# Loading a dense block's u columns and v rows side by side, by one transfer of 8 KB per partition

## The chip, the cores and the metric

The kernel runs on one core of one Trainium2 chip. The time is that of one execution on the device, in microseconds. Three runs of the kernel before gave 4152.92, 4156.69 and 4169.66 us; the median, 4156.69, is the time to which the changed kernel is held.

A core has five engines that take their instructions in order: PE (matmul; PEld is its weight load), DVE (elementwise work), ACT (activation functions, also copies), POOL (here it issues the gathers) and SP (here it issues most loads and stores). Sixteen DMA engines move the data of all queues.

## The reference

A diffusion trunk of two layers runs over 128 context tokens and 512 latent tokens. Each layer normalises, mixes tokens by three parallel head groups, and then lets each token pick single-neuron experts. This case is about the last step, which with its variables shortened reads:

```python
def peer_ffn(h, wq, k1, k2, u, v):                   # u, v: 16384 experts x 1024
    q = (xt @ wq).reshape(n, 8, 128)                 # 8 heads
    s1 = einsum('thd,hnd->thn', q[..., :64], k1)     # 128 keys for each half
    s2 = einsum('thd,hnd->thn', q[..., 64:], k2)
    v1, i1 = top_k(s1, 16); v2, i2 = top_k(s2, 16)
    cand = v1[..., :, None] + v2[..., None, :]       # 256 candidates per head
    top, pos = top_k(cand, 16)
    idx = (i1 * 128 + i2) at pos                     # 16 experts per head and token
    g = softmax(top)
    act = gelu(einsum('td,thkd->thk', x, u[idx]))
    return einsum('thk,thkd->td', g * act, v[idx])
```

So each token reads 128 rows of u and 128 rows of v, chosen by its own data.

## The kernel before

`peer` handles the experts of the 640 tokens in two ways at once. For the first 256 tokens (`TG`) it gathers: for each of the 128 slots a GpSimd indirect DMA (L751) brings 128 rows of 8 KB, one per token, each row an expert's u and v beside each other in the array `uv`. DVE then forms the dot product with the token (L754), ACT the gelu (L756), and DVE adds the weighted v part to `gacc` (L763). There are 4 gather buffers (`NUV`), so a gather can start only when an earlier buffer has been used up by L763.

For the other 384 tokens (`TD`) it is dense: `dense(b)` runs over 128 blocks of 128 experts. It loads the transposed u columns of a block (`raw<-uT`, 512 KB, 4 KB per partition), splits them into a rounded part and a rest (`split`: ACT writes `uhi` in L836, DVE writes `ulo` in L837), and forms all 128 x 384 products on PE (L857 to L859). After gelu (L861) DVE multiplies by the gate array `gres` (L862), which is zero for experts that a token didn't choose. Then it loads the v rows of the block (`raw<-uv`, 512 KB, the second 4 KB of each 8 KB row of `uv`), splits them in the same way into `vhi` and `vlo`, and PE adds the product to `acc` (L877).

Both loads are `dma_start` on SP's queue, into a pool of 4 buffers of 4 KB per partition (`NRAW`), u and v in turn. A load waits until `split` has read the buffer of two blocks ago. The gate array is too large to stay: a stage ahead of the dense loop (`build`, L776 to L802) makes it from one-hot matmuls, keeps a part in `gres` and writes the rest to device memory (`gsp<-sg`, on SP's queue), from where `gres<-gsp` loads on ACT's queue bring it back.

In the dense loop one block and one pump of two gathers alternate (`pump`, `issue_after(gates[...])`). The order on each engine is made by a list scheduler that the framework runs on the program; the pools decide which bytes a tile takes, and a tile waits for the earlier tiles on the same bytes (`reuse_waits="tile"`). `ixT`, `gT` and `iota8` are inputs of `build`: the chosen key indices of the dense tokens, their gates, and a ramp of 128 numbers repeated 8 times.

Of the kernel before, what the change touches and what calls it, by code (L numbers as in the profile page):

```python
# [10 lines left out]
F32 = mybir.dt.float32  # L11
# [4 lines left out]
BF16 = mybir.dt.bfloat16  # L16
F16 = mybir.dt.float16
AF = mybir.ActivationFunctionType
OP = mybir.AluOpType
# [3 lines left out]
D = 1024  # L23
TP, TS = 128, 512
T = TP + TS
L = 2
# [3 lines left out]
NEXP = 16384  # L30
# [14 lines left out]
TD = T - TG  # L45
NT_D = TD // 128
# [6 lines left out]
NUV = 4  # L53
NADA = 2
UAFT = 2
NRAW = 4
NCV = 1
ADAE = 10
ADAP = 3
# [10 lines left out]
class Trunk:  # L70
    def __init__(self, ctx, tc, I, O):
        self.tc, self.nc, self.I, self.O = tc, tc.nc, I, O
        nc = tc.nc
        self.V, self.S, self.G, self.PE = nc.vector, nc.scalar, nc.gpsimd, nc.tensor
        V, S = self.V, self.S
        pers = ctx.enter_context(tc.tile_pool(name="pers", bufs=1))
        consts = pers
        self.xT = xT = pers.tile([128, 8, T], F32, name="xT")
        for k in range(0, 8, 2):
            nc.sync.dma_start(xT[:, k:k + 2, :], I["xT"][k * 128:k * 128 + 256].rearrange("(k p) t -> p k t", p=128))  # L80

        def const(name, shape, dt=F32):
            t = consts.tile(shape, dt, name=name)
            nc.scalar.dma_start(t, I[name])
            return t

        self.vec = const("vec", [128, L, NVEC])
        self.ident = const("ident", [128, 128])
        self.nstep = consts.tile([128, 16], F16, name="nstep16")
        self.thr = consts.tile([128, 2, 16], F16, name="thr16")  # L90
        self.iota = consts.tile([128, 128], BF16, name="iota16")
        self.iota8 = consts.tile([128, 128, 8], BF16, name="iota8")
        self.lmask = consts.tile([128, 7, 128], U8, name="lmask8")
        self.sc = consts.tile([128, 8, 2], F32, name="sc")
        with tc.tile_pool(name="init", bufs=1) as ip:
            for name, shape, dst, dt in (("cT", [128, 8, 2], None, F32), ("lmask", [128, 7, 128], self.lmask, I32),
                                         ("thr", [128, 2, 16], self.thr, F32), ("nstep", [128, 16], self.nstep, F32),
                                         ("iota", [128, 128], self.iota, F32)):
                t = ip.tile(shape, dt, name="i_" + name)
                nc.scalar.dma_start(t, I[name])  # L100
                if dst is None:
                    S.activation(self.sc, t, AF.Silu)
                else:
                    V.tensor_copy(dst, t)
        V.tensor_copy(self.iota8, self.iota[:, :, None].to_broadcast([128, 128, 8]))
        self.eps = consts.tile([128, 1], F32, name="eps")
        V.memset(self.eps, EPS)
        self.one = consts.tile([128, 1], F32, name="one")
        V.memset(self.one, 1.0)
        self.ones = consts.tile([128, 128], F32, name="ones")  # L110
        V.memset(self.ones, 1.0 / D)
        self.identr = consts.tile([128, 128], F32R, name="identr")
        V.tensor_copy(self.identr, self.ident)
        self.ada = [consts.tile([128, 48, 2], F32, name=f"ada{l}") for l in range(L)]
        self.adap = ctx.enter_context(tc.tile_pool(name="adap", bufs=1))
        self.mod = [consts.tile([128, 2, 8, 2], F32, name=f"mod{l}") for l in range(L)]
# [455 lines left out]
    def peer(self, l):  # L572
        tc, nc, I = self.tc, self.nc, self.I
        V, S, G, PE = self.V, self.S, self.G, self.PE
# [4 lines left out]
        gat = self.pool(st, f"gat{l}", side="right")  # L579
        ht = [gat.tile([128, D], F32, name=f"ht{t}") for t in range(2)]  # L580
        gidx = [gat.tile([128, 128], U32, name=f"gidx{t}") for t in range(2)]
        gg = [gat.tile([128, 128], F32, name=f"gg{t}") for t in range(2)]
        ixT = gat.tile([128, 2, TD], BF16, name="ixT")
        gT = gat.tile([128, TD], F32, name="gT")

        self.psj = self.pool(st, f"psjp{l}", 2, PSUM)
        ks = self.pool(st, f"ks{l}", 1)
# [3 lines left out]
        psb = self.pool(f2, f"psbp{l}", 2, PSUM)  # L591
        self.pss = pss = self.pool(f2, f"pssp{l}", 4, PSUM)
        kp = self.pool(f2, f"tk{l}", 1)
        f1 = ExitStack()
        self.wp = self.pool(f1, f"wpp{l}", 2)
        self.tmp = self.pool(f1, f"tmpp{l}", 2)
# [138 lines left out]
        gpool = self.pool(st, f"G{l}", side="right")  # L735
        gres = gpool.tile([128, NR, NTC, GB, TC], F32, name="gres")
        bp = self.pool(f2, f"gb{l}", 2)
        self.wp = bp

        ga = {}  # L740
# [35 lines left out]
        def build(tcn):  # L776
            sg = bp.tile([128, NSP, GB, TC], F32, name="sg", tag="sg")
            for t8 in range(0, TC, 8):
                t0 = tcn * TC + t8
                ohp = bp.tile([128, 8, 128], F32, name="ohp", tag="ohp")  # L780
                ohq = bp.tile([128, 128, 8], BF16, name="ohq", tag="ohq")
                V.tensor_tensor(ohp, ixT[:, 0, t0:t0 + 8, None].to_broadcast([128, 8, 128]),
                                self.iota[:, None, :].to_broadcast([128, 8, 128]), op=OP.is_equal)
                V.tensor_tensor(ohq, ixT[:, 1, None, t0:t0 + 8].to_broadcast([128, 128, 8]), self.iota8, op=OP.is_equal)  # L784
                for t4 in range(0, 8, 4):
                    qg = bp.tile([128, 4, 128], F32, name="qg", tag="qg", bufs=NQG)
                    for t in range(4):
                        S.activation(qg[:, t, :], ohq[:, :, t4 + t], AF.Copy, scale=gT[:, t0 + t4 + t:t0 + t4 + t + 1])  # L788
                    ps = pss.tile([128, 4, 128], F32, name="ps_g", tag="s")
                    for t in range(4):  # L790
                        PE.matmul(ps[:, t, :], qg[:, t, :], ohp[:, t4 + t, :], start=True, stop=True)  # L791
                    tt = t8 + t4
                    S.activation(gres[:, :, tcn, :, tt:tt + 4],
                                 ps[:, :, :NR * GB].rearrange("p t (r b) -> p r b t", r=NR), AF.Copy)
                    so, sp = sg[:, :, :, tt:tt + 4].rearrange("p r b t -> p (r b) t"), ps[:, :, NR * GB:].rearrange("p t b -> p b t")
                    if (tt // 4) % 4 < EVD:
                        V.tensor_copy(so, sp)
                    else:
                        S.activation(so, sp, AF.Copy)  # L799
                for _ in range(NADA):  # L800
                    next(ada, None)
            nc.sync.dma_start(gsp[:, :, tcn].rearrange("r p b t -> p r (b t)"), sg.rearrange("p r b t -> p r (b t)"))  # L802
# [21 lines left out]
        uvp = {n: self.pool(st, f"uv{n}{l}", b) for n, b in (("r", NRAW), ("u", UVB["u"]), ("v", UVB["v"]))}  # L824
        awp = self.pool(st, f"aw{l}", 2)
        acc = pacc.tile([128, NT_D, 2, 512], F32, name="acc")

        def load(src):
            raw = uvp["r"].tile([128, D], F32, name="raw", tag="raw")
            nc.sync.dma_start(raw, src)  # L830
            return raw

        def split(raw, n):
            hi = uvp[n].tile([128, D], F32R, name=n + "hi", tag=n + "hi")
            lo = uvp[n].tile([128, D], F32R, name=n + "lo", tag=n + "lo")
            S.activation(hi, raw, AF.Copy)  # L836
            V.tensor_tensor(lo, raw, hi.bitcast(F32), op=OP.subtract)  # L837
            return hi, lo

        def dense(b):  # L840
            gr, bb = divmod(b, GB)
            nx = gr + NR - 1
            if NR <= nx < NGR and bb % 2 == 0:
# [1 line left out]
                a1 = a0 + 2 * NTC // GB  # L845
                nc.scalar.dma_start(gres[:, nx % NR, a0:a1].rearrange("p a b t -> p (a b t)"),
                                    gsp[nx - NR, :, a0:a1].rearrange("p a b t -> p (a b t)"))
            raw = load(I["uT"][l, b])
            if b >= UAFT:
                with tc.issue_after(gelus[b - UAFT]):  # L850
                    uhi, ulo = split(raw, "u")
            else:
                uhi, ulo = split(raw, "u")
            ps = pa.tile([128, 512], F32, name="ps_a", tag="j")[:, :TD]
            for k in range(8):
                ks = slice(k * 128, k * 128 + 128)
# [5 lines left out]
            gate = V.tensor_tensor(w.rearrange("p (a t) -> p a t", a=NTC), w.rearrange("p (a t) -> p a t", a=NTC),  # L862
                                   gres[:, gr % NR, :, bb, :], op=OP.mult)
            gates.append(gate.ins)
            e0 = l * NEXP + b * 128
            raw = load(I["uv"][e0:e0 + 128, D:])
            whi = awp.tile([128, TD], F32R, name="whi", tag="wh")
            wlo = awp.tile([128, TD], F32R, name="wlo", tag="wl")
            S.activation(whi, w, AF.Copy)  # L869
            V.tensor_tensor(wlo, w, whi.bitcast(F32), op=OP.subtract)  # L870
            vhi, vlo = split(raw, "v")
            parts = ((whi, vhi), (whi, vlo), (wlo, vhi))
            for t in range(NT_D):
                ts = slice(t * 128, t * 128 + 128)
# [16 lines left out]
        for b in range(128):  # L891
# [3 lines left out]
            with tc.issue_after(gates[max(0, b - GLAG)]):  # L895
                while todo and left - len(todo) < left * (b + 1) / 128:
                    pump()
        oa = [uvp["r"].tile([128, D], F32, name="oa", tag="raw") for t in range(NT_D)]
        for t in range(NT_D):
            o = oa[t].rearrange("p (j d) -> p j d", j=2)  # L900
            S.activation(o[:, 0], acc[:, t, 0], AF.Copy)
# [10 lines left out]
def layout(inputs):  # L912
    a = {k: np.ascontiguousarray(np.asarray(v)) for k, v in inputs.items()}
    A = {}
# [20 lines left out]
    s, t = np.arange(128)[:, None], np.arange(128)[None, :]  # L935
# [40 lines left out]
        b = a["na_rpb"][:, :, dr + 7, np.clip(dc, -15, 15) + 15]  # L976
        bias[:, :, :, BOFF[qt][0]:BOFF[qt][0] + kn * 128] = np.where(ok, b, f32(-1e30))
    A["bias"] = bias
    A["uT"] = a["peer_u"].reshape(L, 128, 128, 8, 128).transpose(0, 1, 4, 3, 2).reshape(L, 128, 128, D)
    A["uv"] = np.concatenate([a["peer_u"], a["peer_v"]], -1).reshape(L * NEXP, 2 * D)  # L980
    return {k: np.ascontiguousarray(v) for k, v in A.items()}

# [26 lines left out]
```

## Time and profile before

| what | value |
|---|---|
| median of three runs | 4156.69 us |
| span of the profiled execution, first to last instruction | 4144.4 us (the page gives no other time of it) |
| median less span | 12.3 us |
| PE busy | 3810.6 us, 92% |
| DVE busy | 3333.9 us, 80% |
| ACT busy | 1701.2 us, 41% |
| POOL busy | 757.7 us, 18% |
| moved by DMA | 1011.89 MB in 302267 packets, mean 244 GB/s |
| q0, the gathers | 536.90 MB, 33.5% of 16 DMA engines |
| q1, SP's queue | 425.45 MB, 29.4% |
| q10, ACT's queue | 46.07 MB, 2.8% |

How to read it: the shares are averages over stages of different kinds. Each of the two layers has a mixing and selecting stage and then the dense loop, some 1130 to 1180 us long, in which the DMA engines move about 377 GB/s and PE and DVE both look nearly full. What a change in that loop is worth can only be read from the loop. A packet is what one DMA engine moves at a time, here one partition's row of a transfer.

### The profile page before, as it was taken

What the parts mean: (1) busy time and instruction counts of PE and PEld (TensorE: products, weight loads), DVE (VectorE), ACT (ScalarE), POOL (GpSimd) and SP (SyncE); (2) the same over time, 40 slices, a digit from 0 to 9 for tenths busy, and PEclk for the clock granted to TensorE, in tenths of its full rate; (3) what the DMA queues carried; (4) which work ended last, traced back from release to release, by engine and by line L of the source; (5) the groups of instructions that cost most, each with busy time, mean ns of one, the idle gap of its engine ahead of it and who ended that gap; (6) DMA issues with size and microseconds to landing.
All of it is one profiled execution on the core that took longest, in us unless ns stands there. A gap on an engine that the chain in (4) does not pass through costs nothing.

```text
span 4144.4 us, 54329 instructions
## 1 busy us (share of the span) xinstructions
PE 3810.6 (92%) x19884; PEld 3204.7 (77%) x19884; DVE 3333.9 (80%) x6618; ACT 1701.2 (41%) x3268; POOL 757.7 (18%) x532
## 2 busy tenths in 40 slices
PE   7999997888999999999989999867799999999998
PEld 4896775557888888888878988745688888888886
DVE  4762359788999999999968633988799999999997
ACT  4423332884333333333354243368633333333333
POOL 0000000002333333333300000000133333333331
PEclk8999998998999999999999999978899999999999
DMA  4124232668999999999921221023599999999995
GB/s 161 33 61 128 74 110 68 186 202 291 382 367 387 373 377 375 377 376 379 375 90 33 62 69 57 26 68 113 205 355 383 375 375 372 377 377 377 381 375 213
DMA packets 302267, 1011.89 MB, mean 244 GB/s; under 512 B 28273, under 2 KB 116721, under 8 KB 236209
## 3 DMA queue, kind: packets, MB, share of 16 engines
q0 software_dynamic: 73728, 536.90, 33.5%
q1 hardware_dynamic: 210560, 425.45, 29.4%
q10 hardware_dynamic: 17712, 46.07, 2.8%
q8 instruction: 156, 2.56, 0.2%
q14 instruction: 111, 0.90, 0.1%
HBM read 960.49 MB, written 47.84 MB: 243 GB/s over the span
## 4 chain that ended last, share of the span: by engine, by line
issue 37%; PE 29%; POOL 13%; ACT 9%; DVE 7%; DMA 5%; POOLq 0%; ACTq 0%; DVEq 0%; SPq 0%
PE ps_pj L235 13%; POOL uv L751 13%; ACT qg L788 5%; DMA uv<-uv,gidx 4%; PE ps_ada L162 2%; PE ps_lv L363 2%; PE ps_g L791 2%; PE acc L877 1%; PE npo L529 1%; ACT sg L799 1%; PE ps_s L508 1%; PE ps_ms L187 1%; ACT nt L208 1%; PE po L421 1%; PE pt L524 1%
## 5 line engine op out<-in xcount | busy, mean ns | idle before, releaser
L751 POOL DMA_INDIRECT uv<-uv,gidx x512 | 750.5, 1466 | 3317.0 <-PE ps_g L791 1766.2
L754 DVE SCALAR_TENSOR_TENSOR uv<-uv,ht 128x1024 f32<-128x1024 f32 x512 | 624.2, 1221 | 116.2 <-DMA uv<-uv,gidx 115.4
L859 PE MATMUL ps_a<-hd,ulo 128*128 128x384 f32 x2048 | 695.2, 339 | 17.8 <-DVE ulo L837 17.8
L857 PE MATMUL ps_a<-hd,uhi 128*128 128x384 f32 x2048 | 700.7, 342 | 9.6 <-ACT uhi L836 9.6
L858 PE MATMUL ps_a<-hd,uhi 128*128 128x384 f32 x2048 | 694.0, 339 | 0.0
L763 DVE SCALAR_TENSOR_TENSOR gacc<-uv,gw,gacc 128x1024 f32<-128x1024 f32 x508 | 652.5, 1284 | 15.7
L877 PE MATMUL acc<-vhi,whi 128*128 128x512 f32 x1536 | 506.2, 411 | 67.1 <-ACT whi L869 66.4
L877 PE MATMUL acc<-vhi,wlo 128*128 128x512 f32 x1536 | 486.9, 398 | 2.0 <-DVE wlo L870 1.7
L836 ACT ACTIVATE vhi<-raw 128x1024 fp32r<-128x1024 f32 x256 | 271.6, 1061 | 511.7 <-PE acc L877 496.1
L877 PE MATMUL acc<-vlo,whi 128*128 128x512 f32 x1536 | 480.0, 394 | 0.0
L859 PEld LDWEIGHTS ps_a<-hd,ulo 128*128 128x128 f32 x2048 | 388.3, 190 | 24.9 <-DVE ulo L837 22.7
L857 PEld LDWEIGHTS ps_a<-hd,uhi 128*128 128x128 f32 x2048 | 387.8, 189 | 21.2 <-ACT uhi L836 10.8
L877 PEld LDWEIGHTS acc<-vhi,whi 128*128 128x128 f32 x1536 | 271.6, 189 | 160.4 <-ACT whi L869 113.1
L858 PEld LDWEIGHTS ps_a<-hd,uhi 128*128 128x128 f32 x2048 | 387.7, 189 | 10.0
L788 ACT ACTIVATE qg<-ohq,gT 128x128 f32<-128x128 bf16 x768 | 341.3, 533 | 59.5 <-DVE ohq L784 59.5
L791 PE MATMUL ps_g<-ohp,qg 128*128 128x128 f32 x1536 | 297.9, 338 | 69.5 <-ACT qg L788 68.9
L791 PEld LDWEIGHTS ps_g<-ohp,qg 128*128 128x128 f32 x1536 | 238.4, 221 | 151.9 <-ACT qg L788 116.0
L877 PEld LDWEIGHTS acc<-vhi,wlo 128*128 128x128 f32 x1536 | 282.1, 189 | 81.7 <-DVE wlo L870 24.9
L877 PEld LDWEIGHTS acc<-vlo,whi 128*128 128x128 f32 x1536 | 290.3, 189 | 65.7
L837 DVE TENSOR_TENSOR vlo<-raw,vhi 128x1024 fp32r<-128x1024 f32 x256 | 312.1, 1219 | 13.5 <-ACT vhi L836 13.3
L756 ACT ACTIVATE gw<-dots 128x2 f32<-128x2 f32 x256 | 52.1, 203 | 646.6 <-DVE uv L754 646.4
L837 DVE TENSOR_TENSOR ulo<-raw,uhi 128x1024 fp32r<-128x1024 f32 x256 | 312.8, 1222 | 0.0
(243 smaller groups left out, 6187.5 us busy)
## 6 DMA issues: line engine op xcount, KB each, us to landing
raw<-uT SPq DMA_DIRECT2D x256, 512.0 KB, 6.4
raw<-uv SPq DMA_DIRECT2D x256, 512.0 KB, 8.4
wada<-w_ada SPq DMA_DIRECT2D x192, 256.0 KB, 3.3
gsp<-sg SPq DMA_DIRECT2D x48, 896.0 KB, 5.0
gres<-gsp ACTq DMA_DIRECT2D x112, 384.0 KB, 14.5
wraw<-w_in SPq DMA_DIRECT2D x56, 512.0 KB, 3.6
wraw<-w_out SPq DMA_DIRECT2D x16, 512.0 KB, 3.6
wraw<-wq SPq DMA_DIRECT2D x16, 512.0 KB, 4.0
```

Source lines behind the costliest of these rows:

```text
L235: self.PE.matmul(ps[j][:, :n], w[:, k, :], x[:, k, :], start=(k == 0 and i == 0), stop=(k == 7 and i == 2))
L751: G.indirect_dma_start(out=b, out_offset=None, in_=I["uv"], in_offset=bass.IndirectOffsetOnAxis(ap=gidx[t][:, s:s + 1], axis=0))
L754: V.scalar_tensor_tensor(b[:, :D], b[:, :D], 1.0, ht[t], op0=OP.mult, op1=OP.mult, accum_out=dots[:, s:s + 1])
L763: V.scalar_tensor_tensor(acc_, b[:, D:], w[:, s:s + 1], acc_, op0=OP.mult, op1=OP.add)
L788: S.activation(qg[:, t, :], ohq[:, :, t4 + t], AF.Copy, scale=gT[:, t0 + t4 + t:t0 + t4 + t + 1])
L791: PE.matmul(ps[:, t, :], qg[:, t, :], ohp[:, t4 + t, :], start=True, stop=True)
L836: S.activation(hi, raw, AF.Copy)
L837: V.tensor_tensor(lo, raw, hi.bitcast(F32), op=OP.subtract)
L857: PE.matmul(ps, uhi[:, ks], hd[0][:, k, :], start=(k == 0), stop=False)
L858: PE.matmul(ps, uhi[:, ks], hd[1][:, k, :], start=False, stop=False)
L859: PE.matmul(ps, ulo[:, ks], hd[0][:, k, :], start=False, stop=(k == 7))
L877: PE.matmul(acc[:, t, j, :], a[:, ts], x[:, j * 512:(j + 1) * 512], start=(b == 0 and i == 0), stop=(b == 127 and i == len(parts) - 1))
```

## The change

In device memory the transposed u columns of a block and its v rows are put side by side in a new array `dn`, so that a partition's 4 KB of u and 4 KB of v are one row of 8 KB. `dense` loads both by one transfer of 1 MB into a buffer of 8 KB per partition; there are 3 such buffers in place of 4 of half the size. The gathers still read `uv`.

To make room in SBUF, `iota8` is no longer kept for the whole kernel but made in each layer in a pool of the build stage, and `ixT` and `gT` move from a pool that lives as long as the gathers to one that ends with the build stage.

```diff
-NRAW = 4
+NRAW = 3
...
-        self.iota8 = consts.tile([128, 128, 8], BF16, name="iota8")
...
-        V.tensor_copy(self.iota8, self.iota[:, :, None].to_broadcast([128, 128, 8]))
...
-        ixT = gat.tile([128, 2, TD], BF16, name="ixT")
-        gT = gat.tile([128, TD], F32, name="gT")
...
         kp = self.pool(f2, f"tk{l}", 1)
+        ixT = kp.tile([128, 2, TD], BF16, name="ixT")
+        gT = kp.tile([128, TD], F32, name="gT")
...
         bp = self.pool(f2, f"gb{l}", 2)
+        iota8 = bp.tile([128, 128, 8], BF16, name="iota8", tag="iota8", bufs=1)
+        V.tensor_copy(iota8, self.iota[:, :, None].to_broadcast([128, 128, 8]))
...
-        def load(src):
-            raw = uvp["r"].tile([128, D], F32, name="raw", tag="raw")
-            nc.sync.dma_start(raw, src)
-            return raw
+        def load(b):
+            raw = uvp["r"].tile([128, 2 * D], F32, name="raw", tag="raw")
+            nc.sync.dma_start(raw, I["dn"][l, b])
+            return raw[:, :D], raw[:, D:]
...
-            raw = load(I["uT"][l, b])
+            uraw, vraw = load(b)
...
-            e0 = l * NEXP + b * 128
-            raw = load(I["uv"][e0:e0 + 128, D:])
...
-            vhi, vlo = split(raw, "v")
+            vhi, vlo = split(vraw, "v")
...
-        oa = [uvp["r"].tile([128, D], F32, name="oa", tag="raw") for t in range(NT_D)]
+        oa = [uvp["r"].tile([128, 2 * D], F32, name="oa", tag="raw")[:, :D] for t in range(NT_D)]
...
-    A["uT"] = a["peer_u"].reshape(L, 128, 128, 8, 128).transpose(0, 1, 4, 3, 2).reshape(L, 128, 128, D)
+    uT = a["peer_u"].reshape(L, 128, 128, 8, 128).transpose(0, 1, 4, 3, 2).reshape(L, 128, 128, D)
+    A["dn"] = np.concatenate([uT, a["peer_v"].reshape(L, 128, 128, D)], -1)
```

The scheduler puts some instructions in another place. SP's queue before, at the end of the build stage of layer 0 (`wada<-w_ada` loads weights of the next layer's modulation):

```order
L830 DMA raw<-uT 128x1024
L802 DMA gsp<-sg 128x14x128
L153 DMA wada<-w_ada 128x512 x2
L830 DMA raw<-uv 128x1024
L830 DMA raw<-uT 128x1024
L153 DMA wada<-w_ada 128x512
L830 DMA raw<-uv 128x1024
L153 DMA wada<-w_ada 128x512
L802 DMA gsp<-sg 128x14x128
```

The same end of the stage in the changed kernel:

```order
L802 DMA gsp<-sg 128x14x128
L151 DMA wada<-w_ada 128x512 x4
L802 DMA gsp<-sg 128x14x128
L151 DMA wada<-w_ada 128x512 x2
L802 DMA gsp<-sg 128x14x128 x4
L830 DMA raw<-dn 128x2048
L802 DMA gsp<-sg 128x14x128
L830 DMA raw<-dn 128x2048 x127
```

The first four loads stood ahead of nine stores of gates; now the first load stands ahead of the last store, and the second behind it.

SP's queue before, at the end of the build stage of layer 1:

```order
L600 DMA kk<-keys 128x2048
L216 DMA wraw<-wq 128x1024 x8
L802 DMA gsp<-sg 128x14x128 x16
L830 DMA raw<-uT 128x1024
L830 DMA raw<-uv 128x1024
L830 DMA raw<-uT 128x1024
L830 DMA raw<-uv 128x1024
L802 DMA gsp<-sg 128x14x128 x8
L830 DMA raw<-uT 128x1024
```

The same end in the changed kernel:

```order
L598 DMA kk<-keys 128x2048
L214 DMA wraw<-wq 128x1024 x8
L802 DMA gsp<-sg 128x14x128 x23
L830 DMA raw<-dn 128x2048
L802 DMA gsp<-sg 128x14x128
L830 DMA raw<-dn 128x2048 x127
```

Here, too, the loads of the first two blocks stood eight stores ahead, and now stand around the last store.

DVE before, where the dense loop of layer 0 begins (`m`, `ij`, `pf`, `mk` and `gidx` belong to the selection of the second half of the gathered tokens):

```order
L696 TENSOR_TENSOR m_9109<-mk,dl 128x2048
L837 TENSOR_TENSOR ulo<-raw,uhi 128x1024
L837 TENSOR_TENSOR vlo<-raw,vhi 128x1024
L837 TENSOR_TENSOR ulo<-raw,uhi 128x1024
L837 TENSOR_TENSOR vlo<-raw,vhi 128x1024
L691 TENSOR_TENSOR m_9109<-m_9109 128x128x8
L691 TENSOR_TENSOR m_9109<-m_9109 128x128x4
L691 TENSOR_TENSOR m_9109<-m_9109 128x128x2
L693 TENSOR_TENSOR ij<-m_9109 128x128
L715 TENSOR_TENSOR gidx_4423<-f_9129,ij 128x128
L862 TENSOR_TENSOR w<-w,gres 128x384
```

The same place in the changed kernel:

```order
L689 TENSOR_TENSOR m_9075<-m_9075 128x128x2
L691 TENSOR_TENSOR ij<-m_9075 128x128
L713 TENSOR_TENSOR gidx_4421<-f_9095,ij 128x128
L837 TENSOR_TENSOR ulo<-raw,uhi 128x1024
L837 TENSOR_TENSOR vlo<-raw,vhi 128x1024
L837 TENSOR_TENSOR ulo<-raw,uhi 128x1024
L837 TENSOR_TENSOR vlo<-raw,vhi 128x1024
L862 TENSOR_TENSOR w<-w,gres 128x384
```

The four subtractions of the first two blocks have moved behind the rest of the selection; the first gate multiplication follows either way.

## Rows read from the trace of the kernel before

**Rows 1.** Busy time by stage, inside the dense loops of both layers.

```profile
core 0: us, PE busy (x) PEld busy (x) DVE busy (x) ACT busy (x) POOL busy (x), PEclk, DMA share, GB/s
1200.00:2000.00 800.00, 772.97 (x3789) 678.00 (x3788) 743.76 (x1001) 283.61 (x450) 265.95 (x180) 1.00 0.98 377
3200.00:4000.00 800.00, 770.86 (x3771) 676.44 (x3770) 742.00 (x999) 281.84 (x448) 265.74 (x180) 1.00 0.98 377
```

**Rows 2.** DVE's waits, 1200 to 2000 us, and L754 over the whole span.

```profile
DVE uv L754 <- DMA uv<-uv,gidx: 39.8, 34, 2.9
DVE w L862 <- ACT w L861: 4.7, 20, 1.6
...
L754 DVE SCALAR_TENSOR_TENSOR uv<-uv,ht 128x1024 f32<-128x1024 f32 x512 | 624.2, 1221 | 116.2 <-DMA uv<-uv,gidx 115.4
```

**Rows 3.** DVE in order of time, one block (start, duration, engine, line).

```profile
1504.43 1.22 DVE L837 TENSOR_TENSOR vlo<-raw,vhi 128x1024 fp32r<-128x1024 f32 x1
1505.76 0.56 DVE L862 TENSOR_TENSOR w<-w,gres 128x384 f32<-128x384 f32 x1
...
1512.85 1.22 DVE L837 TENSOR_TENSOR vlo<-raw,vhi 128x1024 fp32r<-128x1024 f32 x1
```

**Rows 4.** DMA queues and issues, 1200 to 2000 us; median us to landing last.

```profile
q0 software_dynamic: 25948, 188.86, 61.0%
q1 hardware_dynamic: 25959, 94.54, 31.1%
q10 hardware_dynamic: 6338, 17.31, 5.5%
...
raw<-uT SPq DMA_DIRECT2D x91, 512.0 KB, 6.5
raw<-uv SPq DMA_DIRECT2D x90, 512.0 KB, 8.6
...
uv<-uv,gidx POOLq DMA_INDIRECT x180, 10.0
```

**Rows 5.** SP's queue, q1, 1504.8 to 1508 us, then 1508.9 to 1513.2 us.

```profile
q1 hardware_dynamic: 147, 0.52, 40.1%
...
q1 hardware_dynamic: 142, 0.53, 36.1%
```

**Rows 6.** SP's and POOL's queues in order of time, around that block.

```profile
1501.87 0.33 SPq L830 DMA_DIRECT2D raw<-uT  x1
1503.46 1.86 POOL L751 DMA_INDIRECT uv<-uv,gidx  x1 [5.26 <-DVE gacc L763]
1505.63 0.93 POOL L751 DMA_INDIRECT uv<-uv,gidx  x1 [0.30 <-issue]
1505.67 0.33 SPq L830 DMA_DIRECT2D raw<-uv  x1
```

**Rows 7.** DMA queues, 1497 to 1498 us, then 1498.6 to 1500 us.

```profile
q1 hardware_dynamic: 95, 0.38, 94.2%
q0 software_dynamic: 12, 0.02, 8.0%
...
q0 software_dynamic: 62, 0.51, 95.0%
q1 hardware_dynamic: 8, 0.02, 4.4%
```

**Rows 8.** Starts of the dense loops: ACT and DVE in order of time.

```profile
961.69 1.06 ACT L836 ACTIVATE vhi<-raw 128x1024 fp32r<-128x1024 f32 x1 [3.71 <-issue]
964.66 1.28 ACT L861 ACT_TABLE_LOAD   x1
969.14 0.56 DVE L862 TENSOR_TENSOR w<-w,gres 128x384 f32<-128x384 f32 x1 [0.47 <-ACT w L861]
...
2962.08 1.06 ACT L836 ACTIVATE vhi<-raw 128x1024 fp32r<-128x1024 f32 x1 [11.38 <-DMA gsp<-sg]
2970.11 0.55 DVE L862 TENSOR_TENSOR w<-w,gres 128x384 f32<-128x384 f32 x1
```

**Rows 9.** The copy into iota8, and two loads by row size.

```profile
L105 DVE COPY iota<-iota x1: 695/695/695, 13.2 to 13.2; 128x1024 bf16<-128x1024 bf16 x1
...
kk<-keys SPq DMA_DIRECT2D x2, 1024.0 KB, 4.9
wraw<-wq SPq DMA_DIRECT2D x16, 512.0 KB, 4.0
```

More of the change, by code (lines that the diff above doesn't have):

```diff
@@ L783, in build @@
                                 self.iota[:, None, :].to_broadcast([128, 8, 128]), op=OP.is_equal)
-                V.tensor_tensor(ohq, ixT[:, 1, None, t0:t0 + 8].to_broadcast([128, 128, 8]), self.iota8, op=OP.is_equal)
+                V.tensor_tensor(ohq, ixT[:, 1, None, t0:t0 + 8].to_broadcast([128, 128, 8]), iota8, op=OP.is_equal)
                 for t4 in range(0, 8, 4):
@@ L847, in dense @@
                                     gsp[nx - NR, :, a0:a1].rearrange("p a b t -> p (a b t)"))
-            raw = load(I["uT"][l, b])
+            uraw, vraw = load(b)
             if b >= UAFT:
                 with tc.issue_after(gelus[b - UAFT]):
-                    uhi, ulo = split(raw, "u")
+                    uhi, ulo = split(uraw, "u")
             else:
-                uhi, ulo = split(raw, "u")
+                uhi, ulo = split(uraw, "u")
             ps = pa.tile([128, 512], F32, name="ps_a", tag="j")[:, :TD]
```

## The prediction, made before the changed kernel was run

> **What bounds the kernel now.** I read the busy times by stage first, since the change touches only the dense loops. In both loops DVE is busy 743 of 800 us, PE 771 to 773 at full granted clock, and the DMA engines 98% of the time at 377 GB/s [rows 1]. Three resources near their end can't be told apart by shares, so the waits come next. DVE, which runs in order, waits for one thing that counts: the gathered rows, 39.8 us in 34 pieces in 800 us, and 115.4 us over both loops; its next wait is 4.7 us [rows 2]. So DVE sets the pace, and the DMA delays it now and then.
>
> One block shows what is left without that delay. From one `vlo` to the next DVE takes 1512.85 - 1504.43 = 8.42 us with hardly a gap [rows 3]. The loop makes 180 gathers in 800 us, two per block [rows 4], so a mean block takes 800 / 90 = 8.89 us. The 0.47 us between are DVE's wait for gathers (39.8 / 90 = 0.44) and small change. That is the most that easier transfers can give: 115.4 us over the kernel. A loop without DMA trouble would be held by DVE at 8.42.
>
> Is the DMA itself full, or do the gathers merely take long? Between issue and landing a gather takes 10.0 us, a u load 6.5, a v load 8.6 [rows 4], while 1 MB at 377 GB/s is moved in 2.8. So all of them stand in line. By queue, in 16 x 800 = 12800 engine us, the gathers use 61.0%, the u and v loads 31.1%, the gates 5.5% [rows 4]: 97.6% together. I take the DMA engines as the resource that makes DVE wait, and price the change by the engine time that it saves there.
>
> **The raw loads in the dense loops.** The u and v rows of the stage take 0.311 x 12800 = 3981 engine us for 94.54 MB, that is for 23081 rows of 4 KB: 172.5 ns each [rows 4]. They are not alike. In a stretch in which one u load was moved, q1 took 0.401 x 16 x 3.2 = 20.5 engine us for 0.52 MB, 162 ns per 4 KB; in the next, with one v load, 0.361 x 16 x 4.3 = 24.8 for 0.53 MB, 192 ns [rows 5]. By the mean of the stage v is then 2 x 172.5 - 162 = 183, and a pair costs 345 ns.
>
> A row of 8 KB on SP's queue doesn't occur in these loops, so its cost is bounded. The nearest row is the u load, which like the new array is read from device memory without holes: twice 162 is 324 ns. The gathers move 8 KB rows, found by index, in 0.61 x 12800 / 23054 = 339 ns [rows 4]. The far end above is two rows of the slow kind, 2 x 192 = 384. The far end below is that the gathers cease to wait at all, -115 us for the kernel. I take 324, because the v rows lose their stride.
>
> Each engine moves 8 of the 128 rows of a transfer, so a block saves 8 x (345 - 324) = 0.17 us of each engine's time, and 256 blocks 43 us. At 339 ns it would be 8 x 6 = 0.05 us, 12 us in all; at 384 a loss of 0.31 us per block, 80 us. As long as DVE waits for gathers that stand in line, time saved on the engines shortens the wait by as much; 0.17 is well under the 0.44 that there is to take.
>
> **Issue and buffers.** SP issues one transfer fewer per block, 0.33 us [rows 6]; SP only waits for buffers here, so this is worth nothing. Before, u was reloaded after `ulo` and v after `vlo`, two blocks ahead; now both go after `vlo`, three blocks ahead. The row is needed about two block times later, some 17 us, against landings of 6.5 and 8.6 us. So ACT shouldn't wait for it. Splitting, matmuls, gates and pumps are as many and as long as before, and their order on DVE in the steady loop is the same up to the neighbourhood of `select(1)` in layer 1, to which I give no cost.
>
> **The start of each loop.** Before, four loads lay ready when the build stage ended, and `vhi` of block 0 started when the last store of gates let go of its bytes, at 961.69 and 2962.08 us [rows 8]. Now the first load of 1 MB stands just ahead of that store and the second behind it. Each costs 2.8 us of transfer at 377 GB/s. So `vhi` of block 0 comes 2.8 us later (964.5), the second load lands 2.8 us after that (967.3), and then follow two splits on ACT of 1.06 us, the table load of 1.28 and the gelu of some 0.5: the first gate multiplication is ready at 971.2 instead of 969.14, 2 us late. DVE's four subtractions have moved behind the selection work and so fill the wait. In layer 1 the same sum from 2962.08 gives 971.6 against 970.11 after the thousands, 1.5 us late. `iota8` is copied twice, 0.7 us each [rows 9], instead of once at the beginning, where DVE was idle: 1.4 us at most. Together 5 us. The bounds are 0 (the scheduler's reordering covers all) and twice that sum, 10, if stores and gathers share the engines with the loads.
>
> **Sum.** -43 + 5 = -38 us. The profiled execution has a span of 4144.4 us and the median of the runs is 4156.69, 12.3 us more for what lies around the span and for the spread of runs; I keep that difference. 4144.4 - 38 + 12.3 = 4119 us.
>
> **The rivals.**
> *The merged row is no cheaper than a gathered one (339 ns).* Then 12 us are saved, 5 lost: 4150 us. For it: the gathers read whole 8 KB rows and are still slower per byte than u. The v load also competes with both gathers issued at 1503.46 and 1505.63, u rather less [rows 6], so its 192 ns may be due to its place in time, which the new load inherits: it is issued where v was.
>
> *The gathers stop waiting.* If the slow v rows also slow the gathers, and one interruption per block is easier than two, most of the 115.4 us goes: -75 to -110, 4047 to 4082 us. DVE's 8.42 us per block is the end. For it: 56 of 90 blocks already run without a wait. Against: the engines would have to move the same bytes in 5% less time.
>
> *The longer transfer holds back the gathers: slower.* In one microsecond q1 has 94.2% of the engines and the gathers 8.0%; a little later the gathers have 95.0% and q1 4.4% [rows 7]. The queues take turns by whole runs of rows, not row by row. A raw load's run is now 8 x 324 = 2.6 us instead of 1.3. A gather that is last in its pair, and late, then lands 1.3 us later. Where this hits only waiting blocks (34 of 90, so 97 of 256) it costs up to 126 us, less the other gather of the block, which is not interrupted any more; half of it, 63, less the 38 saved, gives 4182 us. It decides if the new load regularly begins between the two gathers of a pair and the engines idle later in the block; while they stay 98% busy, the order in line can't change the mean. [...]
>
> **How the numbers follow.** A difference of 0.5%, 21 us, is about what a measurement of this kernel can tell from no change. Forecast (4119, by its own bounds 4095 to 4140): 46%, of which nine tenths are faster by more than that. No cheaper row (4150): 27%, nearly all within it. No waiting gathers (4047 to 4082): 13%, all faster. Held back gathers (4182, from 4150 to 4220): 14%, two thirds of it slower. That gives faster 0.58, within 0.31, slower 0.11. The range leaves out the better half of the third case and the worse part of the last: 4062 to 4172.
>
> **What would show it.** In the changed profile q1 should take 29 to 30% of the engines in the loop where it took 31.1, at a higher GB/s; some 324 ns per 8 KB row; DVE's wait for gathers should fall from 39.8 to about 25 us in 800 us; landings of gathers should be shorter. If rows cost 339 ns or more, the second case holds. If gathers land later than 10.0 us and DVE waits more, the last one does. If `uhi` waits for a load in the steady loop, my account of the buffers is wrong. The first gate multiplication should come 2 us later in each loop.

## The result and the profile after

The changed kernel took 4129.88 us (median of four runs, 4128.05 to 4136.37) against 4157.34 us of the kernel before on the same chip. The ratio is 0.9941, with a 95% interval of 0.9925 to 0.9958: some 27 us, 0.6% faster. The forecast was 4119 us and faster, so sign and range held; the gain is some seven tenths of the 38 us forecast.

Busy time inside both loops, as in [rows 1]:

```profile
1200.00:2000.00 800.00, 779.07 (x3837) 685.82 (x3836) 752.76 (x1010) 285.09 (x456) 263.62 (x182) 1.00 0.97 382
3200.00:4000.00 800.00, 777.96 (x3814) 685.43 (x3813) 749.55 (x1007) 283.79 (x454) 263.98 (x182) 0.99 0.96 379
```

PE and DVE are busier by 6 to 9 us in 800, the DMA engines a little less busy at a higher rate. Two more gathers were made in the same time (182 against 180).

DVE's waits for gathers, 1200 to 2000 us, and L754 over the whole span; below them ACT's waits in the same stretch (us, times, longest):

```profile
DVE uv L754 <- DMA uv<-uv,gidx: 29.5, 26, 3.4
...
L754 DVE SCALAR_TENSOR_TENSOR uv<-uv,ht 128x1024 f32<-128x1024 f32 x512 | 623.5, 1220 | 84.4 <-DMA uv<-uv,gidx 83.6
```

```profile
ACT gw L756 <- DVE uv L754: 222.2, 91, 6.6
ACT vhi L836 <- PE acc L875: 181.5, 89, 2.3
ACT w L861 <- PE ps_a L859: 96.8, 90, 4.2
ACT whi L867 <- DVE w L862: 15.5, 15, 3.0
```

The wait that was to fall fell: 39.8 to 29.5 us in 800 us, 115.4 to 83.6 over the kernel [rows 2]. No `uhi` waits for a load, as three buffers were to ensure.

The queues of the same stretch, as in [rows 4]:

```profile
q0 software_dynamic: 26329, 191.71, 62.5%
q1 hardware_dynamic: 13158, 95.87, 28.5%
```

A row of 8 KB on SP's queue costs 0.285 x 12800 us / 11703 = 312 ns; the pair of 4 KB rows cost 345. The gathers' rows cost 342 ns, 3 more than before. q1 takes 28.5% of the engines, where 29 to 30% were foreseen. How long the gathers took to land, this trace doesn't show.

Where the time is, by the first and last gate multiplication of each loop (start, duration), first of the changed kernel, then the two of the kernel before that don't stand in [rows 8]:

```profile
976.46 0.56 DVE L862 TENSOR_TENSOR w<-w,gres 128x384 f32<-128x384 f32 x1 [0.94 <-ACT w L861]
2095.67 0.56 DVE L862 TENSOR_TENSOR w<-w,gres 128x384 f32<-128x384 f32 x1
2972.72 0.55 DVE L862 TENSOR_TENSOR w<-w,gres 128x384 f32<-128x384 f32 x1
4089.03 0.56 DVE L862 TENSOR_TENSOR w<-w,gres 128x384 f32<-128x384 f32 x1
```

```profile
2097.34 0.56 DVE L862 TENSOR_TENSOR w<-w,gres 128x384 f32<-128x384 f32 x1
...
4106.03 0.56 DVE L862 TENSOR_TENSOR w<-w,gres 128x384 f32<-128x384 f32 x1
```

Up to the first gate the changed kernel loses 7.3 us, in the first loop it gains 9.0, between the loops it loses 4.3, in the second it gains 19.6; behind the last gate both need 38.4. That is -17.0 us, the difference of the two spans (4144.4 and 4127.4). The medians differ by 27: the profiled execution of before was one of its quicker ones (its runs lay between 4143 and 4170 us). Parts of under some 10 us in a single profile are therefore not read as effects unless several traces show them.

### The profile page after: what moved, and what is told of

It is laid out like the page before. It is cut to its first block, busy times and chain, and to the rows that moved or that the text cites. A ratio compares the mean times of both kernels' runs of the same rounds, so it can differ in the third digit from the quotient of the medians.

```text
span 4127.4 us, 53267 instructions
## 1 busy us (share of the span) xinstructions
PE 3806.6 (92%) x19884; PEld 3206.3 (78%) x19884; DVE 3336.6 (81%) x6619; ACT 1697.7 (41%) x3268; POOL 753.5 (18%) x532
## 4 chain that ended last, share of the span: by engine, by line
issue 34%; PE 33%; POOL 11%; ACT 9%; DVE 7%; DMA 6%; POOLq 0%; ACTq 0%; SPq 0%; DVEq 0%
PE ps_pj L233 13%; POOL uv L751 11%; DMA uv<-uv,gidx 5%; ACT qg L788 5%; PE acc L875 3%; PE ps_ada L160 3%; PE ps_lv L361 2%; PE ps_g L791 2%; PE npo L527 1%; ACT sg L799 1%; PE ps_ms L185 1%; PE ps_s L506 1%; PE ps_a L857 1%; PE ps_a L858 1%; PE ps_a L859 1%
## 5 line engine op out<-in xcount | busy, mean ns | idle before, releaser
L754 DVE SCALAR_TENSOR_TENSOR uv<-uv,ht 128x1024 f32<-128x1024 f32 x512 | 623.5, 1220 | 84.4 <-DMA uv<-uv,gidx 83.6
L763 DVE SCALAR_TENSOR_TENSOR gacc<-uv,gw,gacc 128x1024 f32<-128x1024 f32 x508 | 652.5, 1284 | 16.1
L858 PEld LDWEIGHTS ps_a<-hd,uhi 128*128 128x128 f32 x2048 | 386.5, 189 | 10.1
```

The costliest lines, as they stand in the source:

```text
L754: V.scalar_tensor_tensor(b[:, :D], b[:, :D], 1.0, ht[t], op0=OP.mult, op1=OP.mult, accum_out=dots[:, s:s + 1])
L763: V.scalar_tensor_tensor(acc_, b[:, D:], w[:, s:s + 1], acc_, op0=OP.mult, op1=OP.add)
L858: PE.matmul(ps, uhi[:, ks], hd[1][:, k, :], start=False, stop=False)
```

## The experiments

Each was timed beside the kernel before on the same chip. The ratios are to those runs, whose medians lay between 4153.72 and 4157.34 us.

| kernel | us | ratio, 95% interval | SP pair of rows, ns | DVE waits for gathers, us in all |
|---|---|---|---|---|
| before | 4157.34 | 1 | 345 | 115.4 |
| changed | 4129.88 | 0.9941, 0.9925 to 0.9958 | 312 | 83.6 |
| v rows without holes, nothing else | 4124.52 | 0.9935, 0.9918 to 0.9951 | 325 | 79.7 |
| SBUF edits, nothing else | 4163.94 | 1.0020, 1.0006 to 1.0034 | 345 | 127.9 |
| changed, 1 MB made of 4 KB rows | 4127.94 | 0.9940, 0.9926 to 0.9954 | 323 | 81.3 |
| changed, two loads of strided halves | 4214.31 | 1.0136, 1.0114 to 1.0158 | 361 | 182.1 |
| v rows 4.5 KB apart | 4118.59 | 0.9921, 0.9905 to 0.9936 | 326 | 81.3 |
| v rows 8.5 KB apart | 4119.58 | 0.9911, 0.9894 to 0.9929 | 325 | 79.6 |
| changed, half the load | 4063.32 | 0.9774, 0.9761 to 0.9787 | - | 29.3 |
| plain v rows, SBUF edits, 5 gather buffers | 4048.51 | 0.9746, 0.9734 to 0.9759 | 326 | 0.4 |
| strided v rows, SBUF edits, 5 gather buffers | 4053.87 | 0.9759, 0.9743 to 0.9774 | 344 | 3.2 |
| changed, 2 raw buffers | 4177.14 | 1.0058, 1.0044 to 1.0071 | 312 | 20.2 |
| changed, 2 raw and 5 gather buffers | 4188.05 | 1.0078, 1.0062 to 1.0094 | 313 | 0.0 |

The pair is q1's share of 12800 engine us divided by the number of 8 KB that it moved, 1200 to 2000 us, as above; the last column is the wait of L754 in one profiled execution.

**v rows without holes.**

```diff
-            raw = load(I["uv"][e0:e0 + 128, D:])
+            raw = load(I["vr"][l, b])
```

> The kernel before with one edit: the v rows are read from an array of their own without holes, in place of every second 4 KB of the gathers' array. Transfers, buffers and order stay. Theory 'stride' (a 4 KB row costs more when the rows lie 8 KB apart): a v row falls from some 184 ns to the 163 ns of a u row, so 8 x 21 = 0.17 us of engine time per block, 43 us over 256 blocks; the changed kernel turned 68 us of engine time into 29 us of loop time, so 43 become some 18: 4139 us. Rival 'place in time' (v is slower because it runs beside both gathers of its block): a v row stays near 184 ns and the time within 5 us of the kernel before, 4157. Rival 'row size' (only longer rows help): the same, 4157.

SP's queue and the landings in this kernel, 1200 to 2000 us:

```profile
q1 hardware_dynamic: 26228, 95.48, 29.6%
...
raw<-uT SPq DMA_DIRECT2D x92, 512.0 KB, 5.5
raw<-vr SPq DMA_DIRECT2D x91, 512.0 KB, 7.7
uv<-uv,gidx POOLq DMA_INDIRECT x182, 8.3
```

The pair costs 325 ns, so a v row now costs what a u row does, and the time is 4124.52 us: all of the change's gain, by another source address alone. "Stride" holds, though the time is better than the 4139 that it gave; "place in time" and "row size" fall, since transfers, order and rows' length stayed. All three landings are shorter [rows 4]: gathers 8.3 against 10.0 us.

**Two loads of strided halves.**

```diff
-            nc.sync.dma_start(raw, I["dn"][l, b])
+            for i in range(2):
+                nc.sync.dma_start(raw[:, i * D:i * D + D], I["dn"][l, b, :, i * D:i * D + D])
```

> The changed kernel, with the same array and the same 3 buffers, but the u half and the v half loaded by a transfer of 512 KB each, issued one behind the other: 4 KB rows that lie 8 KB apart, u and v both. Theory 'stride': both rows cost some 184 ns, 368 the pair against 345 before, 0.18 us more engine time per block, 47 us in all; DVE's wait for gathers rises above the 116 us of the kernel before, and with the late starts the time is 4157 + 12 + 20 to 47 = 4190 to 4215. Rival 'place in time': u and v rows cost about the same as before or less, 4157 to 4170. Rival 'one transfer for two': the gain is gone and no more, 4157 to 4170; it doesn't foresee u rows above 163 ns.

```profile
q1 hardware_dynamic: 25202, 91.79, 31.6%
...
uv<-uv,gidx POOLq DMA_INDIRECT x175, 10.8
...
L754 DVE SCALAR_TENSOR_TENSOR uv<-uv,ht 128x1024 f32<-128x1024 f32 x512 | 624.0, 1220 | 183.2 <-DMA uv<-uv,gidx 182.1
```

Now u has the distance of 8 KB too; the pair costs 361 ns and the time rises to 4214.31 us. The same theory seen from the other side: this kernel, with 16 ns more a pair than before, is 59 us slower (with the SBUF edits, priced below); those with some 20 ns less are 27 to 37 us faster. How much of the 59 is the stride's isn't shown: both loads of a block go out together here, and no run did that with plain rows. But the pair's cost speaks against a rival, that v was dear because the gathers read the same array: `dn` is read by these loads alone.

**One transfer made of 4 KB rows.**

```diff
-            nc.sync.dma_start(raw, I["dn"][l, b])
+            nc.sync.dma_start(raw.rearrange("p (a d) -> p a d", a=2), I["dn"][l, b].rearrange("a p d -> p a d"))
...
-    A["dn"] = np.concatenate([uT, a["peer_v"].reshape(L, 128, 128, D)], -1)
+    A["dn"] = np.stack([uT, a["peer_v"].reshape(L, 128, 128, D)], 2)
```

> The changed kernel, still one transfer of 1 MB into the same 3 buffers, but u and v of a block lie one behind the other in device memory, so that the transfer is made of 256 rows of 4 KB without holes in place of 128 rows of 8 KB. Theory 'stride' alone: the pair costs 2 x 163 = 326 ns against 312 of one 8 KB row and 345 before; of the 68 us of engine time some 39 are still saved, and by the same conversion (0.43) the time is 4130 + 12 = 4142 us. Rival 'row size' (the 8 KB row is what helps): the pair costs 345 or more, 4157 plus the late starts, 4168. Rival 'one transfer for two' (the number of transfers helps): as the changed kernel, 4130.

```profile
q1 hardware_dynamic: 24767, 95.49, 29.4%
...
raw<-dn SPq DMA_DIRECT2D x90, 1024.0 KB, 10.2
uv<-uv,gidx POOLq DMA_INDIRECT x182, 9.3
```

The pair costs 323 ns, and the time, 4127.94 us, is that of the changed kernel, better than the 4142 that "stride" gave and near the 4130 of "one transfer for two". The 8 KB row's further 11 ns (312 against 323) are real on the engines and worth nothing in time. But fewer transfers show no gain either: from the first to the last gate multiplication, both loops together took 2264.1 us before and between 2234.2 and 2237.0 in the five kernels with a pair of 312 to 326 ns and four gather buffers, two with one transfer per block and three with two plain loads.

**Which distance costs.** The v rows alone again, with holes behind them of 512 bytes, then of 4.5 KB.

```diff
+    A["vr"] = np.pad(a["peer_v"].reshape(L, 128, 128, D), ((0, 0), (0, 0), (0, 0), (0, 128)))
```

> The kernel before with the v rows in an array of their own, as in the run with plain v rows, but with a hole of 512 bytes behind each row of 4 KB, so that rows begin 4.5 KB apart. Theory 'holes' (the row costs more as soon as the next one does not follow on): a v row costs 184 ns as before, and the time is 4150 to 4160. Rival 'the distance of 8 KB' (rows that all begin on a multiple of 8 KB, so that only one half of each 8 KB of memory is read, are served more slowly): the v row costs 163 to 170 ns, and the time is that of plain v rows, 4120 to 4130.

> The run with the 512 byte holes again, now with holes of 4.5 KB, so that rows of 4 KB begin 8.5 KB apart. Theory 'a distance of 8 KB' (what costs is that all rows begin at the same place of an 8 KB step of memory): the v row costs some 163 ns, 4115 to 4130. Rival 'large holes' (any hole as large as the row costs): 184 ns, 4150 to 4160.

SP's queue, first with rows 4.5 KB apart, then 8.5 KB apart:

```profile
q1 hardware_dynamic: 26354, 95.96, 29.8%
```

```profile
q1 hardware_dynamic: 26361, 95.97, 29.7%
```

326 and 325 ns a pair, and both times are at least as good as without holes. So holes as such cost nothing, small or large; of the distances that were run (4, 4.5, 8 and 8.5 KB) only 8 KB costs. Why it costs more there no run here shows.

**SBUF edits alone.** `iota8`, `ixT` and `gT` as in the changed kernel, loads as before.

> The kernel before with only the edits in SBUF: iota8 made in each layer in the build stage's pool, ixT and gT in the selection's pool. The loads stay two of 512 KB, 4 buffers of 4 KB, v rows with their stride. Theory 'the late starts belong to the moves' (the first gate multiplication came 7.3 us later in layer 0, and the stretch between the loops grew by 4.3 us in the changed kernel): both appear here, the loops cost 8.88 us a block as before, 4157 + 12 = 4169 us. Rival 'the late starts belong to the 1 MB transfer': no late start, 4157 us. Open beside it: 14 of the 29 us that the loops gained came in the first 32 blocks of layer 1. If the moved order of the selection gave them, the first 32 blocks take some 280 us here too and the time is 4155; if the lighter loads gave them, they take 294.

Its first gate multiplication:

```profile
976.62 0.56 DVE L862 TENSOR_TENSOR w<-w,gres 128x384 f32<-128x384 f32 x1
```

The late start of layer 0 is there without any 1 MB load. In the nine kernels with these edits the first gate came between 972.7 and 981.0 us, in the four without between 969.1 and 971.7. The time is 8 us longer (2 to 14). Between the loops, the four without took 870.0 to 876.6 us and those with the edits 871.8 to 878.7. The ranges overlap, but their middle values, 872.1 and 876.9, lie 5 us apart, as much as the 4.3 us above: that the edits cost something there too is likely and not shown. The first 32 blocks of layer 1 took 300 us here and 294 before, 280 and 281 in the two kernels with one transfer of all the rows, and 290 to 293 in the three with two plain loads. So that part of the gain goes with the one transfer; what makes it was not tested, and layer 0 shows nothing like it.

**Half the load.** What is left when the DMA engines have room? This kernel leaves out the v rows.

```diff
-            nc.sync.dma_start(raw, I["dn"][l, b])
-            return raw[:, :D], raw[:, D:]
+            nc.sync.dma_start(raw[:, :D], I["dn"][l, b, :, :D])
+            return raw[:, :D], raw[:, :D]
```

> The changed kernel, but only the u half of a row is loaded (512 KB per block, 4 KB rows 8 KB apart), and the v split reads this half again: the v rows of the dense tokens are left out of the load, all instructions on the engines stay. It takes some 8 x 130 = 1.0 us of DMA engine time out of each block and asks what the loops cost when the DMA engines have room. Theory 'the engines are what is full' (what is left of DVE's wait for gathers, 84 us, is standing in line): the wait falls below 25 us, the DMA share of the loops to some 87%, and a block costs what DVE or PE need, between 8.42 and 8.56 us against 8.77: 44 to 80 us less, 4050 to 4086. Rival 'the gathers' own way is too long for 4 buffers' (issue, 16 rows of 342 ns on each engine and landing, whoever else is in line): half of the wait stays, 4100 or more.

```profile
1200.00:2000.00 800.00, 796.52 (x3949) 707.36 (x3948) 773.90 (x1041) 292.55 (x469) 267.56 (x188) 1.00 0.88 330
...
DMA to landing us min/median/max: 6.1/8.4/11.9
```

The wait falls to 29.3 us, not quite below 25, and the time to 4063.32; PE is busy 796.5 of 800 us: behind DVE's waits PE is the next limit. The time is what "the engines are full" foresaw, and its rival gave 4100 or more. But the gathers land earlier as well (median 8.4 us, the latest 11.9), so this run can't tell full engines from gathers that are late for their use.

**A fifth gather buffer.** With the SBUF edits, in the bytes that the changed kernel gives to its raw rows; first with plain v rows, then with strided ones.

```diff
-NUV = 4
+NUV = 5
```

> The kernel before with the v rows in an array without holes, the edits in SBUF, and the bytes these free used for a fifth gather buffer; two loads of 512 KB as before. Theory 'the engines are what is full': a pair of raw rows costs 325 ns, the engines' time of a block is 16 x 342 + 8 x 325 + 490 = 8.56 us, and one more buffer changes nothing in it: 4124 of the kernel with plain v rows plus the 8 us of the edits in SBUF, 4120 to 4140. Rival 'too few gather buffers': each gather may be issued half a block earlier (4.3 us, against waits that are 3.4 us at the longest), DVE's wait falls from 80 to below 25 us, and the time to 4070 to 4085.

> The kernel before with the edits in SBUF and the fifth gather buffer alone: the v rows keep their distance of 8 KB, two loads of 512 KB. Theory 'deadline' (a gather is late when its landing exceeds what lies between the freeing of its buffer and its use; the fifth buffer adds half a block to that, and then the cost of a raw row matters little): DVE's wait for gathers stays below 15 us over the kernel, a block costs some 8.5 us, and the time is 4050 to 4065. Rival 'engine time' (the rows' time on the engines adds up to what a block can't go below: 16 x 339 + 8 x 345 + 490 = 8.67 us against 8.48 of the run with plain v rows and five buffers): 0.19 x 256 = 49 us above that run's 4048, 4090 to 4105.

Both take the gathers' wait away. With plain rows the time is 4048.51 us, below even the 4070 to 4085 of "too few gather buffers". The strided one decides between deadline and engine time: 4053.87 us, not 4090. Its loop of layer 0, its landing of gathers, and L754:

```profile
1200.00:2000.00 800.00, 798.17 (x3970) 711.59 (x3970) 777.95 (x1048) 293.41 (x471) 264.12 (x188) 1.00 1.00 394
...
uv<-uv,gidx POOLq DMA_INDIRECT x188, 10.7
...
L754 DVE SCALAR_TENSOR_TENSOR uv<-uv,ht 128x1024 f32<-128x1024 f32 x512 | 622.2, 1219 | 3.5 <-DMA uv<-uv,gidx 3.2
```

Gathers land later than in the kernel before (10.7 against 10.0 us), the engines are busy 100%, and DVE waits 3.2 us instead of 115.4. So neither the share nor the landing by itself made DVE wait; what counts is how long a gather may take. In the changed kernel, issue of two gathers on POOL and the dot products on DVE that use them:

```profile
1500.91 1.86 POOL L751 DMA_INDIRECT uv<-uv,gidx  x1 [4.75 <-DVE gacc L763]
1503.08 0.94 POOL L751 DMA_INDIRECT uv<-uv,gidx  x1 [0.30 <-issue]
...
1512.10 1.21 DVE L754 SCALAR_TENSOR_TENSOR uv<-uv,ht 128x1024 f32<-128x1024 f32 x1
1513.71 1.21 DVE L754 SCALAR_TENSOR_TENSOR uv<-uv,ht 128x1024 f32<-128x1024 f32 x1
```

And with five buffers and plain rows:

```profile
1440.97 1.86 POOL L751 DMA_INDIRECT uv<-uv,gidx  x1 [3.61 <-DVE gacc L763]
1443.14 0.93 POOL L751 DMA_INDIRECT uv<-uv,gidx  x1 [0.30 <-issue]
...
1453.84 1.22 DVE L754 SCALAR_TENSOR_TENSOR uv<-uv,ht 128x1024 f32<-128x1024 f32 x1
...
1460.68 1.22 DVE L754 SCALAR_TENSOR_TENSOR uv<-uv,ht 128x1024 f32<-128x1024 f32 x1
```

With four buffers the issue waits for L763, and from then on the two gathers have 11.2 and 10.6 us. With five they have 12.9 and 17.5. The landings of the kernel before, 1200 to 2000 us:

```profile
DMA to landing us min/median/max: 6.6/10.0/13.8
```

Of its 180 gathers there, by the landings in the trace, 66 took longer than 10.6 us, 36 longer than 11.2, 13 longer than 12.9, and none 17.5. Of the 34 waits in [rows 2], 33 are for the second gather of a pair, the one with the shorter time.

**Two raw buffers.** With four gather buffers, then with five.

```diff
-NRAW = 3
+NRAW = 2
```

> The changed kernel with 2 raw buffers of 8 KB in place of 3 (as many bytes as the kernel before had; the last tiles that share the pool lie two in a buffer). A load is then issued two blocks ahead, when vlo has read the buffer, and its u half is needed some 8 us later. Theory 'the third buffer is needed': a 1 MB load stands in line for 8 us or more (512 KB took 6.5 and 8.6 before), uhi waits for it in most blocks by 1 to 2 us, some of it reaches PE and DVE, and the time is 4180 to 4400. Rival 'two are enough' (ACT has slack: it waits 180 us per 800 us for PE before vhi): uhi waits, DVE doesn't, and the time stays at 4125 to 4140.

> The changed kernel with the bytes of its third raw buffer given to a fifth gather buffer (2 of 8 KB for the raw rows, 5 for the gathers). Theory 'two deadlines' (with 2 buffers the 1 MB load lands too late for uhi, 45 times in 800 us and for 34 us, and this is no matter of the gathers): the loops cost what they cost with 2 raw and 4 gather buffers or somewhat less, 4130 to 4180. Rival 'the fifth gather buffer heals it' (what matters is that gathers are issued early, whatever stands beside them): 4050 to 4090.

ACT's and PE's waits with two raw and five gather buffers, 1200 to 2000 us:

```profile
ACT uhi L836 <- DMA raw<-dn: 34.2, 41, 2.0
...
PE acc L875 <- ACT whi L867: 32.2, 39, 1.9
```

`uhi` is late in nearly half of the blocks, PE gets it passed on through `whi`, and the time is 23 and 32 us above the kernel before: just below the range that "the third buffer is needed" gave for the first, above the one given for the second. The fifth gather buffer takes the gathers' wait to zero and brings nothing: the raw rows' deadline then holds the loop. The third buffer of 8 KB is needed.

## Why the prediction was right, and where its sizes were off

**The cause was named rightly.** "The v rows lose their stride" is the whole gain: it appears with nothing else changed, and the loops of the kernels that also merge the loads are no shorter. That u before was the plain row and v the dear one, 162 and 183 ns, was read from [rows 4, 5], and the two plain rows cost 325 ns where 324 was taken. The merged row itself costs 312, a saving of 8 x 33 ns = 0.26 us per block instead of 0.17.

**The term that failed is the conversion.** The prediction said that "time saved on the engines shortens the wait by as much". 0.26 us over 256 blocks are 68 us; the wait fell by 31.8 and the loops by 28.6. Nor is the rate constant: with plain v rows, 20 ns less a pair are 41 us, and the loops fell by 27.1; the next 13 ns, from 325 to 312, brought nothing. That the forecast came so near is partly luck, since a saving taken too small (43 for 68 us) met a conversion taken too large (1 for 0.42). It took the DMA engines as the resource because they were 98% busy [rows 1]. The runs show in its place a deadline of 10.6 to 11.2 us, set by four buffers: lighter rows make some late gathers punctual, and earlier than punctual brought little: with five buffers, plain v rows let gathers land after 9.2 us instead of 10.7 and gave 0.9746 instead of 0.9759. (Why the last 13 ns helped none of the gathers that were still late, 26 in 800 us, stays open.) The engines were no limit at 98%: the same transfers ran at 394 GB/s in place of 377 once a fifth buffer was there, 4.5% more, while the busy share, at 98%, left room for 2% at most.

**The start was priced too low.** 5 us were put down for both layers. Layer 0 alone lost 7.3 us in this profile. The working there took the first store's end from the old trace, but the build stage itself comes out later with the moved tiles. ACT's last write to `sg` there, before, with the SBUF edits alone, and in the changed kernel:

```profile
956.50 0.54 ACT L799 ACTIVATE sg<-ps_g 128x448 f32<-128x448 f32 x1
...
961.59 0.54 ACT L799 ACTIVATE sg<-ps_g 128x448 f32<-128x448 f32 x1
...
961.61 0.54 ACT L799 ACTIVATE sg<-ps_g 128x448 f32<-128x448 f32 x1
```

Behind it, in the changed kernel:

```profile
966.67 1.06 ACT L836 ACTIVATE uhi<-raw 128x1024 fp32r<-128x1024 f32 x1 [4.51 <-DMA raw<-dn]
969.77 1.06 ACT L836 ACTIVATE vhi<-raw 128x1024 fp32r<-128x1024 f32 x1 [2.05 <-DMA gsp<-sg]
972.07 1.06 ACT L836 ACTIVATE uhi<-raw 128x1024 fp32r<-128x1024 f32 x1 [1.24 <-DMA raw<-dn]
```

The chain is the one described, load, store, load; it only begins later: `vhi` runs at 969.77 instead of the 964.5 foreseen.

**Two smaller points.** The 12.3 us kept between span and median were mostly the spread of runs; in the changed kernel a run of 4129.16 us has a span of 4127.4. And 0.33 us less issue on SP showed no gain, as said: the loops with two plain loads are no longer.

**The rivals.** The merged row is cheaper than a gathered one (312 against 342 ns), so the second case falls. Gathers that cease to wait were not this change's doing, but the price put on it was right: a fifth buffer (with the SBUF edits, the rows as strided as before) gave -102 us, within the -75 to -110, and its loops take 8.47 and 8.49 us a block where DVE's 8.42 was called the end. The held back gathers are half there: with the same 4 KB rows, one transfer of 1 MB let gathers land after 9.3 us, two of 512 KB after 8.3 (the SBUF edits, which only the first had, leave the landing at 10.1 where it was 10.0). It did not decide, since DVE waited as much in both (81.3 and 79.7 us).

## What to carry to other kernels

Before pricing a transfer by its share of busy engines, measure from the issue to the use of what is waited for: if that time is fixed by the number of buffers, one more buffer can be worth more than cheaper rows. Here the change spent freed SBUF on raw rows and won 27 us; the same bytes as a fifth gather buffer win 102, with plain v rows 105 (4048.51 us, below both kernels), and PE is then busy 798.6 of 800 us. Rows of 4 KB that lie 8 KB apart (181 ns each here, against 163) deserve an array of their own, or a distance of 4.5 or 8.5 KB; others were not tried.

## What was not expected of the hardware

- 4 KB rows that begin 8 KB apart cost some 181 ns each (361 the pair); 4.5 and 8.5 KB apart they cost 163, as they do without holes. With half the load, where only u halves of `dn` are read, they cost 0.184 x 12800 / 12034 = 196 ns, by the first row below.
- The time of a gathered 8 KB row is elastic: 339 ns with four buffers at 377 GB/s [rows 4], 0.619 x 12800 / 24222 = 327 ns with five at 394 and strided v rows, by the second row below. So the busy time that the profile gives for a DMA engine is no fixed price of the bytes.

```profile
q1 hardware_dynamic: 13536, 49.29, 18.4%
```

```profile
q0 software_dynamic: 27259, 198.42, 61.9%
```
